# Queries and keys of a hybrid decoder layer written straight to both heads' operands, and the first attention weights issued among the first pair's projections

## The chip, the cores and the metric

One NeuronCore of a Trainium2 chip runs the kernel. The metric is the device time of one execution in microseconds (us), shown as the median of three runs; one further execution was profiled.

## The reference, cut to what matters

One decoder layer on 1024 tokens with model width 1024, all in float32: a joint input projection whose columns feed a short gated convolution, stick-breaking attention (8 heads of 64) and a spatial gating unit; an output projection; a squared-ReLU MLP; a gated per-layer embedding. The change touches the attention alone:

```python
q = rms_norm(q.reshape(bsz, s_len, ATTN_HEADS, HEAD_DIM), q_norm_g[i])
k = rms_norm(k.reshape(bsz, s_len, ATTN_HEADS, HEAD_DIM), k_norm_g[i])
...
z = jnp.einsum('bqhd,bkhd->bhqk', qi, kj) * scale
log_beta = jax.nn.log_sigmoid(z)
log_rem = jnp.where(causal, jax.nn.log_sigmoid(-z), 0.0)
suffix = lax.cumsum(log_rem, axis=3, reverse=True) - log_rem
weights = jnp.where(causal, jnp.exp(log_beta + suffix), 0.0)
o = jnp.einsum('bhqk,bkhd->bqhd', weights, vj)
```

## The kernel before

**Precision.** Each float32 operand of a matmul is kept as a high part and a low part in the type float32r. A product of two such operands takes three matmuls (high by high, high by low, low by high; lines 161 to 163). Most work outside TensorE is the making of these parts: ScalarE casts the high part (line 134, or line 137 with a gain), VectorE subtracts it for the low part (line 135 or 138).

**Stages.** The kernel first brings the inputs and normalises them (the tiles xn), runs the gating unit's projection (`gating`, tiles vu_ps), then the attention's projections and the attention itself, mixed with one another and later with the convolution's projections (cv_ps); then the output projection (o_ps, from 410.7 us of the profile), the MLP (f_ps, d_ps) and the gate (g_ps). The heads go in four pairs. `project(pr)` makes q, k and v of one pair of heads: eight token tiles t of 128, each with 24 matmuls into the bank qkv_ps, then ScalarE and VectorE work (sum of squares ss, the root rs on GpSimd, the product qk, and V's two parts).

**Turning.** After each second tile `turn_qk` (lines 395 to 419) transposes q and k of two tiles and both heads into one PSUM bank qk_tr, head 0 on partitions 0 to 63 (lo_p), head 1 on 64 to 127 (hi_p). The operands that the attention wants, per head hh and half th of the tokens, are QS (q's high part on the head's own partitions, its low part on the other 64), KH (k's high part on both) and KL (k's low part on the head's own, zeros elsewhere), so that z = q k takes two matmuls with 128 rows each. Before the change the turn writes q's high part of both heads into QS[0], its low part into q_lo, k's high part into KH[0], and both KL. After the fourth tile of a half (t % 4 == 3) six joins move 64-partition pieces: three on ScalarE (lines 413 to 415), three on VectorE (lines 416 to 418). Until then neither head has its operands.

**Attention.** `attention()` yields 32 steps, for each pair head 0 with the token groups g = 0 to 3 and then head 1 with g = 3 to 0. A step has two parts. `stick` makes two tiles of weights: z by TensorE (lines 448, 450), a sigmoid by ScalarE into rem (line 452), a product scan along the keys by VectorE (line 457), and differences wt on VectorE or GpSimd (line 464); the lengths go from 128 to 1024 with the token tile, so the steps with g = 3 are the heavy ones, and they stand next to each other in the middle of a pair. `gather` transposes the weights (w_tr, line 486), splits them into wT_hi and wT_lo, and multiplies with V into the bank av (line 504). qk_tr, w_tr and a few others share a pool of three PSUM banks (ps_tr).

**Order.** The order of issue is written with generators: `weave` takes from the attention and from the next projections (`fill`) by their units of work, `later` delays a turn by 72 units. A scheduler of the Tile framework then moves instructions within an engine's queue; each engine runs its queue in order. Before the change the attention starts when `alone`, the gating unit and the first pair's projections, has been written out whole (lines 697 to 706).

Of the kernel before, what the change touches and what calls it, by code (L numbers as in the profile page):

```python
# [17 lines left out]
KT = D // P  # L18
# [15 lines left out]
def hybrid_block(ctx: ExitStack, tc: tile.TileContext, a: dict):  # L34
# [310 lines left out]
    def project(pr):  # L345
# [9 lines left out]
        low_q = [None, None]  # L355
        heads[pr] = QS, KH, KL, V, low_q
        for t in range(KT):
            th, ts = block(t)
            if t % 4 == 0:
                for hh, other in enumerate((hi_p, lo_p)):  # L360
                    KL[hh][th] = slot("KL", F32R)
                    nc.gpsimd.memset(KL[hh][th][other].bitcast(F32), 0.0)
                KH[0][th] = slot("KH", F32R)
                QS[0][th] = slot("QS", F32R)
                low_q[th] = slot("q_lo", F32R)
                QS[1][th] = slot("QS", F32R)
                KH[1][th] = slot("KH", F32R)
# [27 lines left out]
    def turn_qk(head, t, qk):  # L395

        QS, KH, KL, _, low_q = head
# [7 lines left out]

        split(tr[:, :256], QS[0][th][:, ws], low_q[th][:, ws], scale=gq)
        nc.scalar.activation(KH[0][th][:, ws], tr[:, 256:], AF.Copy, scale=gk)
        for hh, own in enumerate((lo_p, hi_p)):
            nc.vector.scalar_tensor_tensor(out=KL[hh][th][own, ws], in0=tr[own, 256:],
                                           scalar=gk[own], in1=KH[0][th][own, ws],  # L410
                                           op0=ALU.mult, op1=ALU.subtract)
        if t % 4 == 3:
            nc.scalar.copy(KH[1][th][hi_p], KH[0][th][hi_p])
            nc.scalar.copy(KH[1][th][lo_p], KH[0][th][hi_p])
            nc.scalar.copy(KH[0][th][hi_p], KH[0][th][lo_p])
            nc.vector.tensor_copy(QS[1][th][hi_p], QS[0][th][hi_p])
            nc.vector.tensor_copy(QS[1][th][lo_p], low_q[th][hi_p])
            nc.vector.tensor_copy(QS[0][th][hi_p], low_q[th][lo_p])
# [4 lines left out]
    def attend(pr):  # L423

        QS, KH, KL, V, _ = heads[pr]
# [203 lines left out]


# [67 lines left out]
    fill = stream(project(1), project(2), project(3), convolve())  # L698
    for _ in alone:
        pass  # L700
    attending = attention()
    for pr in range(4):
        while waiting:
            emitted[0] += waiting.pop(0)[1]()
        weave(attending, ATTEND + {0: AHEAD, 3: -AHEAD}.get(pr, 0), fill,
              PROJECT if pr < 3 else CONVOLVE * 0.72)
# [638 lines left out]
```

## Time and profile before

| | |
|---|---|
| median of three runs | 1207.83 us (1206.86 to 1211.2) |
| the profiled execution's own time | 1206.75 us |
| its span | 1205.0 us |
| TensorE's granted clock | at its full level in all 40 slices |
| TensorE busy | 1181.0 us, 98% |
| VectorE, ScalarE, GpSimd busy | 885.7, 595.5, 400.5 us |
| projections and attention, mixed | about 75 to 410 us |

The span is what the profiler saw from the first to the last instruction; the execution's own time is 1.75 us longer. A busy TensorE counts overlapping matmuls, so that its idle time is a lower bound of what it lost. Each view names, for an engine's idle time, the instruction that ended it ("releaser").

### The profile page before, as it was taken

The numbers are of one execution on the slowest core, as the hardware profiler recorded it, in microseconds if no ns is written. First come the engines' busy times: TensorE is split into PE (matmuls) and PEld (weight loads), VectorE is DVE, ScalarE is ACT, GpSimd is POOL, SyncE is SP. The second block draws the span as 40 slices with busy tenths as digits, with TensorE's granted clock in tenths as the row PEclk, the third lists the DMA queues.
The fourth block names the chain that finished last, engine by engine and source line by source line (L and its number), as shares of the span: only waits on it lengthen the run. The fifth ranks groups of instructions, "written<-read, shape, count | busy, mean of one in ns | idle before, by whom it ended". The sixth has DMA issues, their size and how long they took to land.

```text
span 1205.0 us, 17538 instructions
## 1 busy us (share of the span) xinstructions
PE 1181.0 (98%) x5788; PEld 1007.1 (84%) x5788; DVE 885.7 (73%) x1310; ACT 595.5 (49%) x1148; POOL 400.5 (33%) x472
## 2 busy tenths in 40 slices
PE   9999899998999999999999999999999999999997
PEld 7899899898888888888888888888888888888886
DVE  7846898989896667868877777787664657753697
ACT  7735565565643466733334333356543444456642
POOL 3324355464352222045354453421023301013412
PEclk9999999999999999999999999999999999999999
DMA  9602359999673776679998989777889975644857
GB/s 311 233 18 90 130 172 262 253 194 167 140 146 95 196 263 204 204 207 261 265 240 249 264 238 260 221 257 277 300 267 295 290 249 175 231 146 119 181 155 209
DMA packets 127963, 254.03 MB, mean 211 GB/s; under 512 B 14496, under 2 KB 22432, under 8 KB 127168
## 3 DMA queue, kind: packets, MB, share of 16 engines
q1 hardware_dynamic: 94992, 168.08, 41.4%
q0 software_dynamic: 27664, 57.05, 25.2%
q10 hardware_dynamic: 5216, 27.79, 6.4%
q8 instruction: 45, 0.74, 0.3%
q14 instruction: 46, 0.38, 0.1%
HBM read 192.30 MB, written 92.80 MB: 237 GB/s over the span
## 4 chain that ended last, share of the span: by engine, by line
PE 88%; DVE 8%; ACT 1%; issue 1%; DMA 1%; POOL 1%; SPq 0%; DVEq 0%; ACTq 0%; POOLq 0%
PE f_ps L814 25%; PE d_ps L814 25%; PE g_ps L814 6%; DVE rem L457 3%; PE qkv_ps L161 3%; PE qkv_ps L162 2%; PE qkv_ps L163 2%; PE o_ps L161 2%; PE o_ps L163 2%; PE o_ps L162 2%; PE av L504 2%; PE cv_ps L163 2%; PE cv_ps L161 2%; PE cv_ps L162 2%; PE w_tr L486 1%; PE vu_ps L162 1%
## 5 line engine op out<-in xcount | busy, mean ns | idle before, releaser
L135 DVE TENSOR_TENSOR w_lo<-raw,w_hi 128x512 fp32r<-128x512 f32 x280 | 243.1, 872 | 85.0 <-ACT w_hi L134 83.1
L134 ACT CAST w_hi<-raw 128x512 fp32r<-128x512 f32 x280 | 172.5, 620 | 240.5 <-PE d_ps L814 115.4
L814 PE MATMUL f_ps<-hn_hi,w_hi 128*128 128x512 f32 x448 | 175.2, 392 | 0.0
L814 PE MATMUL f_ps<-hn_lo,w_hi 128*128 128x512 f32 x448 | 174.9, 390 | 0.0
L814 PE MATMUL d_ps<-f_hi,w_hi 128*128 128x512 f32 x448 | 174.8, 390 | 0.0
L814 PE MATMUL f_ps<-hn_hi,w_lo 128*128 128x512 f32 x448 | 174.6, 391 | 0.0
L814 PE MATMUL d_ps<-f_hi,w_lo 128*128 128x512 f32 x448 | 174.3, 389 | 0.0
L814 PE MATMUL d_ps<-f_lo,w_hi 128*128 128x512 f32 x448 | 174.3, 389 | 0.0
L457 DVE TENSOR_TENSOR_SCAN rem<-rem,after 128x128 f32<-128x128 f32 (+3 forms) x64 | 90.9, 1431 | 13.3 <-ACT rem L452 13.3
L814 PEld LDWEIGHTS f_ps<-hn_lo,w_hi 128*128 128x128 f32 x448 | 84.5, 189 | 17.9 <-issue 0.2
L814 PEld LDWEIGHTS f_ps<-hn_hi,w_hi 128*128 128x128 f32 x448 | 84.5, 189 | 17.8 <-issue 0.2
L814 PEld LDWEIGHTS f_ps<-hn_hi,w_lo 128*128 128x128 f32 x448 | 84.5, 189 | 17.6
L814 PEld LDWEIGHTS d_ps<-f_hi,w_hi 128*128 128x128 f32 x448 | 84.1, 188 | 17.7 <-issue 0.2
L814 PEld LDWEIGHTS d_ps<-f_hi,w_lo 128*128 128x128 f32 x448 | 84.1, 188 | 17.6
L814 PEld LDWEIGHTS d_ps<-f_lo,w_hi 128*128 128x128 f32 x448 | 84.1, 188 | 17.5 <-issue 0.2
L161 PE MATMUL qkv_ps<-whi,xn_hi 128*128 128x384 f32 x256 | 88.8, 347 | 0.9 <-DVE V L138 0.8
L162 PE MATMUL qkv_ps<-wlo,xn_hi 128*128 128x384 f32 x256 | 86.6, 338 | 0.0
L163 PE MATMUL qkv_ps<-whi,xn_lo 128*128 128x384 f32 x256 | 86.3, 337 | 0.0
L135 DVE TENSOR_TENSOR f_lo<-raw,f_hi 128x512 fp32r<-128x512 f32 x112 | 78.2, 728 | 8.5 <-ACT f_hi L134 8.2
L134 ACT CAST f_hi<-raw 128x512 fp32r<-128x512 f32 x112 | 67.1, 620 | 25.6 <-DMA raw<-f_dram 21.6
L800 POOL TENSOR_TENSOR S<-S,sq 128x512 f32<-128x512 f32 x19 | 25.6, 1347 | 160.1 <-ACT sq L876 160.1
L452 ACT ACTIVATE rem<-z 128x128 f32<-128x128 f32 (+3 forms) x96 | 46.7, 500 | 24.3 <-PE z L450 21.6
(250 smaller groups left out, 2618.9 us busy)
## 6 DMA issues: line engine op xcount, KB each, us to landing
raw<-in_w_ff SPq DMA_DIRECT2D x148, 256.0 KB, 4.2
raw<-f_dram SPq DMA_DIRECT2D x112, 256.0 KB, 5.1
raw<-w_sums SPq DMA_DIRECT2D x64, 256.0 KB, 4.1
f_dram<-f SPq DMA_DIRECT2D x48, 256.0 KB, 3.9
f_dram<-t SPq DMA_DIRECT2D x48, 256.0 KB, 4.0
w_sums<-in_w_ff POOLq DMA_DIRECT2D x8, 1024.0 KB, 12.1
w_sums<-w_sums POOLq DMA_DIRECT2D x8, 1024.0 KB, 15.3
raw<-in_w_out SPq DMA_DIRECT2D x28, 256.0 KB, 3.5
```

Source lines behind the costliest of these rows:

```text
L134: last_hi[0] = nc.scalar.copy(hi, src)
L135: low.tensor_tensor(out=lo, in0=src, in1=hi, op=ALU.subtract)
L161: nc.tensor.matmul(ps, lh, rh, start=first and i == 0, stop=False)
L162: nc.tensor.matmul(ps, lh, rl, start=False, stop=False)
L163: done = nc.tensor.matmul(ps, ll, rh, start=False, stop=last and i == len(terms) - 1)
L452: last_act[0] = nc.scalar.activation(rem[:, ks], z, AF.Sigmoid, scale=-HD ** -0.5)
L457: nc.vector.tensor_tensor_scan(out=back, data0=back, data1=after[:, T - W:][:, ::-1], initial=1.0, op0=ALU.mult, op1=ALU.max)
L486: nc.tensor.transpose(tr[:, n:n + P], wts[i][:, kb * P:(kb + 1) * P], ident)
L504: nc.tensor.matmul(av[:, first * P:], lhs, part[:, o:o + m], start=kb == 0 and part is hi, stop=kb == 2 * g + 1 and part is lo)
L800: return eng.tensor_tensor(out=out, in0=x, in1=y, op=ALU.add)
L814: done = nc.tensor.matmul(bank, l, r, start=first and k == 0 and i == 0, stop=k == len(b) - 1 and i == 2, skip_group_check=True)
```

## The change

The q and k parts are written by six ScalarE and four VectorE instructions per turn, each on the 64 partitions of one head, straight to the places where the attention reads them: for each head q's high part to QS's own half, k's high part to KH's own half, q's low part to QS's other half, k's low part to KL, and k's high part once more to KH's other half. The tile q_lo and the six joins are gone. The first step's `stick` (26 units) is taken when 100 units of the first pair's projections are left, instead of behind them, and `weave`'s totals follow.

```diff
--- before.py
+++ after.py
@@ -352,19 +352,16 @@
         KH = [[None, None], [None, None]]
         KL = [[None, None], [None, None]]
         V = [None] * 4
-        low_q = [None, None]
-        heads[pr] = QS, KH, KL, V, low_q
+        heads[pr] = QS, KH, KL, V
         for t in range(KT):
             th, ts = block(t)
             if t % 4 == 0:
                 for hh, other in enumerate((hi_p, lo_p)):
                     KL[hh][th] = slot("KL", F32R)
                     nc.gpsimd.memset(KL[hh][th][other].bitcast(F32), 0.0)
-                KH[0][th] = slot("KH", F32R)
-                QS[0][th] = slot("QS", F32R)
-                low_q[th] = slot("q_lo", F32R)
-                QS[1][th] = slot("QS", F32R)
-                KH[1][th] = slot("KH", F32R)
+                for hh in range(2):
+                    QS[hh][th] = slot("QS", F32R)
+                    KH[hh][th] = slot("KH", F32R)
             ps = bank(ps_mm, "qkv_ps")[:, :384]
             for k0 in range(0, KT, 2):
                 product(ps, [(cols(xn[k][th], ts), wk[k]) for k in (k0, k0 + 1)],
@@ -394,7 +391,7 @@
 
     def turn_qk(head, t, qk):
 
-        QS, KH, KL, _, low_q = head
+        QS, KH, KL, _ = head
         th = t // 4
         tr = bank(ps_tr, "qk_tr")
         for i in range(2):
@@ -402,27 +399,22 @@
                 o = j * 256 + i * P
                 nc.tensor.transpose(tr[:, o:o + P], qk[:, i, j * P:(j + 1) * P], ident)
         ws = slice((t % 4 - 1) * P, (t % 4 + 1) * P)
-
-        split(tr[:, :256], QS[0][th][:, ws], low_q[th][:, ws], scale=gq)
-        nc.scalar.activation(KH[0][th][:, ws], tr[:, 256:], AF.Copy, scale=gk)
-        for hh, own in enumerate((lo_p, hi_p)):
-            nc.vector.scalar_tensor_tensor(out=KL[hh][th][own, ws], in0=tr[own, 256:],
-                                           scalar=gk[own], in1=KH[0][th][own, ws],
-                                           op0=ALU.mult, op1=ALU.subtract)
-        if t % 4 == 3:
-            nc.scalar.copy(KH[1][th][hi_p], KH[0][th][hi_p])
-            nc.scalar.copy(KH[1][th][lo_p], KH[0][th][hi_p])
-            nc.scalar.copy(KH[0][th][hi_p], KH[0][th][lo_p])
-            nc.vector.tensor_copy(QS[1][th][hi_p], QS[0][th][hi_p])
-            nc.vector.tensor_copy(QS[1][th][lo_p], low_q[th][hi_p])
-            nc.vector.tensor_copy(QS[0][th][hi_p], low_q[th][lo_p])
+        for hh, (own, other) in enumerate(((lo_p, hi_p), (hi_p, lo_p))):
+            q, k = tr[own, :256], tr[own, 256:]
+            nc.scalar.activation(QS[hh][th][own, ws], q, AF.Copy, scale=gq[own])
+            nc.scalar.activation(KH[hh][th][own, ws], k, AF.Copy, scale=gk[own])
+            nc.vector.scalar_tensor_tensor(out=QS[hh][th][other, ws], in0=q, scalar=gq[own],
+                                           in1=QS[hh][th][own, ws], op0=ALU.mult, op1=ALU.subtract)
+            nc.vector.scalar_tensor_tensor(out=KL[hh][th][own, ws], in0=k, scalar=gk[own],
+                                           in1=KH[hh][th][own, ws], op0=ALU.mult, op1=ALU.subtract)
+            nc.scalar.activation(KH[hh][th][other, ws], k, AF.Copy, scale=gk[own])
         return 8
 
     PROJECT = KT * 72 + 32
 
     def attend(pr):
 
-        QS, KH, KL, V, _ = heads[pr]
+        QS, KH, KL, V = heads[pr]
         yb = y_kept if pr == 3 else None
         if pr == 3:
             y_kept.extend(halves("y_b"))
@@ -627,6 +619,8 @@
             if t % 4 == 3:
                 later(250, lambda th=th, vp=vp, vu=vus: mix(th, vp, vu))
 
+    GATING = 2 * (4 * KT * 12 + 1 + 24 + 16)
+
 
     y_a = []
 
@@ -696,13 +690,18 @@
         pass
     alone = stream(gating(), project(0))
     fill = stream(project(1), project(2), project(3), convolve())
+
+    for _ in take(alone, GATING + PROJECT - 100):
+        pass
+    attending = attention()
+    for _ in take(attending, AHEAD):
+        pass
     for _ in alone:
         pass
-    attending = attention()
     for pr in range(4):
         while waiting:
             emitted[0] += waiting.pop(0)[1]()
-        weave(attending, ATTEND + {0: AHEAD, 3: -AHEAD}.get(pr, 0), fill,
+        weave(attending, ATTEND - (AHEAD if pr == 3 else 0), fill,
               PROJECT if pr < 3 else CONVOLVE * 0.72)
     y = [[], []]
 
```

The scheduler makes more of this than the diff tells. Three places show it. In all rows the number behind a tile's name tells tiles of one name apart.

On TensorE, in the first pair's projections (qkv_ps, 24 matmuls a tile), behind the fifth of their eight tiles: before, the transposes of the third and fourth tile (qk_tr) are followed by the sixth tile's projections, and the first z stand behind the seventh tile.

```order
L163 MATMUL qkv_ps_1161<-whi_945,xn_lo_524 128x384
L403 MATMUL qk_tr_1186<-ident,qk_1062 128x128 x4
L161 MATMUL qkv_ps_1214<-whi_903,xn_hi_462 128x384
L162 MATMUL qkv_ps_1214<-wlo_904,xn_hi_462 128x384
L163 MATMUL qkv_ps_1214<-whi_903,xn_lo_463 128x384
```
```order
L163 MATMUL qkv_ps_1249<-whi_945,xn_lo_524 128x384
L448 MATMUL z_1349<-KH_953,QS_954 128x128
L450 MATMUL z_1349<-KL_949,QS_954 128x128
L448 MATMUL z_1422<-KH_953,QS_954 128x256
L450 MATMUL z_1422<-KL_949,QS_954 128x256
L403 MATMUL qk_tr_1274<-ident,qk_1209 128x128 x2
```

Now:

```order
L163 MATMUL qkv_ps_1164<-whi_945,xn_lo_524 128x384
L440 MATMUL z_1278<-KH_954,QS_953 128x128
L442 MATMUL z_1278<-KL_949,QS_953 128x128
L400 MATMUL qk_tr_1189<-ident,qk_1061 128x128 x2
L440 MATMUL z_1287<-KH_954,QS_953 128x256
L442 MATMUL z_1287<-KL_949,QS_953 128x256
L400 MATMUL qk_tr_1189<-ident,qk_1061 128x128 x2
L161 MATMUL qkv_ps_1216<-whi_903,xn_hi_462 128x384
```

The first z of head 0 moved from behind the seventh tile to behind the fifth, in among the transposes of the third and fourth tile, whose joins they no longer need.

On TensorE, in the first pair's heavy steps, around the transposes of head 0's longest weights (w_tr of wt_1587 before, wt_1586 now): before, no projection stands in the 24 rows between their own z and them; the last two z in that piece, shown here, are head 1's.

```order
L448 MATMUL z_1722<-KH_957,QS_1159 128x512
L450 MATMUL z_1722<-KL_951,QS_1159 128x512
L486 MATMUL w_tr_1735<-ident,wt_1587 128x128
L486 MATMUL w_tr_1735<-ident,wt_1568 128x128
L486 MATMUL w_tr_1735<-ident,wt_1587 128x128
L486 MATMUL w_tr_1750<-ident,wt_1587 128x128
L486 MATMUL w_tr_1750<-ident,wt_1568 128x128
L486 MATMUL w_tr_1750<-ident,wt_1587 128x128
L448 MATMUL z_1835<-KH_1160,QS_1159 128x128
L450 MATMUL z_1835<-KL_1154,QS_1159 128x128
L448 MATMUL z_1839<-KH_957,QS_1159 128x512
L450 MATMUL z_1839<-KL_951,QS_1159 128x512
```

Now 20 projections of one tile, 12 matmuls of av, four z of head 1 and four more projections stand between head 0's z and these transposes; the end of that piece:

```order
L442 MATMUL z_1675<-KL_1158,QS_1162 128x384
L440 MATMUL z_1679<-KH_956,QS_1162 128x512
L442 MATMUL z_1679<-KL_951,QS_1162 128x512
L163 MATMUL qkv_ps_1623<-whi_1427,xn_lo_397 128x384
L161 MATMUL qkv_ps_1623<-whi_1433,xn_hi_429 128x384
L162 MATMUL qkv_ps_1623<-wlo_1434,xn_hi_429 128x384
L163 MATMUL qkv_ps_1623<-whi_1433,xn_lo_430 128x384
L400 MATMUL qk_tr_1705<-ident,qk_1530 128x128 x2
L478 MATMUL w_tr_1739<-ident,wt_1567 128x128
L478 MATMUL w_tr_1754<-ident,wt_1567 128x128
L478 MATMUL w_tr_1739<-ident,wt_1586 128x128
L478 MATMUL w_tr_1739<-ident,wt_1567 128x128
```

Projections (qkv_ps) moved in between the heavy steps; head 1's longest z moved behind the transposes.

On VectorE, at the same place, the turn of the second pair's first two tiles, with the instruction ahead of it:

```order
L457 SCALAR_TENSOR_TENSOR rem_1586<-rem_1586,after 128x1024
L138 SCALAR_TENSOR_TENSOR q_lo_1410<-qk_tr_1672,c_gq,QS_1409 128x256
L384 TENSOR_TENSOR qk_1704<-qkv_ps_1709,rs_1783 128x256
L464 TENSOR_TENSOR wt_1587<-rem_1586 128x1023
L457 SCALAR_TENSOR_TENSOR rem_1684<-rem_1684,after 128x896
L409 SCALAR_TENSOR_TENSOR KL_1404<-qk_tr_1672,c_gk,KH_1408 64x256
L409 SCALAR_TENSOR_TENSOR KL_1406<-qk_tr_1672,c_gk,KH_1408 64x256
```

Now:

```order
L135 TENSOR_TENSOR wT_lo_1745<-w_tr_1739,wT_hi_1744 128x512
L406 SCALAR_TENSOR_TENSOR QS_1441<-qk_tr_1705,c_gq,QS_1441 64x256
L408 SCALAR_TENSOR_TENSOR KL_1437<-qk_tr_1705,c_gk,KH_1442 64x256
L135 TENSOR_TENSOR wT_lo_1760<-w_tr_1754,wT_hi_1759 128x512
L381 TENSOR_TENSOR qk_1727<-qkv_ps_1623,rs_1725 128x256
L449 SCALAR_TENSOR_TENSOR rem_1692<-rem_1692,after 128x1024
L406 SCALAR_TENSOR_TENSOR QS_1443<-qk_tr_1705,c_gq,QS_1443 64x256
L408 SCALAR_TENSOR_TENSOR KL_1439<-qk_tr_1705,c_gk,KH_1444 64x256
```

The turn has two halves, one per head, with other work between them; a scan of 1024 moved between the halves, and the difference wt of 1023 out of them.

## Rows read from the trace of the kernel before

**Rows 1.** The page, part 1: busy time and instructions of each engine.
```profile
PE 1181.0 (98%) x5788; PEld 1007.1 (84%) x5788; DVE 885.7 (73%) x1310; ACT 595.5 (49%) x1148; POOL 400.5 (33%) x472
```

**Rows 2.** What TensorE waited for, 85 to 400 us: total us, times, longest.
```profile
PE w_tr L486 <- DVE KL L409: 3.6, 4, 1.5
PE w_tr L486 <- DVE wt L464: 3.2, 3, 1.6
PE av L504 <- DVE wT_lo L135: 2.9, 4, 1.8
PE qk_tr L403 <- DVE qk L384: 1.5, 1, 1.5
```

**Rows 3.** Busy time by stretch of 20 to 25 us: first stretch, sum of all fifteen.
```profile
85.00:110.00 25.00, 25.00 (x157) 24.87 (x156) 12.44 (x33) 10.05 (x26) 6.17 (x9) 1.00 0.06 22
...
sum 305.00, PE 291.68 PEld 268.61 DVE 258.22 ACT 165.83 POOL 145.30; mean PE 19.45 PEld 17.91 DVE 17.21 ACT 11.06 POOL 9.69
```

**Rows 4.** Busy time in three stretches with the longest scans, and in a calm one.
```profile
129.60:166.00 36.40, 32.98 (x206) 30.21 (x205) 32.02 (x41) 18.35 (x44) 12.51 (x15) 1.00 0.36 123
196.00:232.40 36.40, 33.86 (x215) 31.26 (x213) 32.45 (x42) 18.78 (x45) 17.52 (x18) 1.00 0.95 244
261.00:298.00 37.00, 33.72 (x211) 31.10 (x212) 33.07 (x42) 19.38 (x47) 16.93 (x20) 1.00 1.03 190
...
232.40:261.00 28.60, 28.56 (x193) 27.74 (x193) 25.72 (x47) 19.31 (x51) 20.48 (x33) 1.00 0.85 207
```

**Rows 5.** Timeline of TensorE, 140 to 152 us: start, length, what ended idle time.
```profile
141.96 0.60 PE L403 MATMUL qk_tr<-ident,qk 128*128 128x128 f32 x4
...
147.02 0.88 PE L486 MATMUL w_tr<-ident,wt 128*128 128x128 f32 x6 [1.64 <-DVE wt L464]
...
149.93 0.63 PE L486 MATMUL w_tr<-ident,wt 128*128 128x128 f32 x4 [0.94 <-DVE KL L409]
```

**Rows 6.** VectorE's groups by form, 85 to 400 us: busy us, mean ns, idle before.
```profile
L135 DVE TENSOR_TENSOR wT_lo<-w_tr,wT_hi 128x512 fp32r<-128x512 f32 x48 | 32.1, 680 | 3.4 <-ACT wT_hi L134 2.7
...
L457 DVE TENSOR_TENSOR_SCAN rem<-rem,after 128x1024 f32<-128x1024 f32 x8 | 19.2, 2403 | 1.7 <-ACT rem L452 1.7
...
L409 DVE SCALAR_TENSOR_TENSOR KL<-qk_tr,c_gk,KH 64x256 fp32r<-64x256 f32 x32 | 15.3, 479 | 1.5 <-ACT KH L407 1.1
L384 DVE TENSOR_TENSOR qk<-qkv_ps,rs 128x256 f32<-128x256 f32 x31 | 12.9, 415 | 8.9 <-POOL rs L170 8.7
...
L464 DVE TENSOR_TENSOR wt<-rem 128x1023 f32<-128x1023 f32 x8 | 10.5, 1312 | 0.0
...
L138 DVE SCALAR_TENSOR_TENSOR q_lo<-qk_tr,c_gq,QS 128x256 fp32r<-128x256 f32 x16 | 7.5, 471 | 0.6 <-ACT QS L137 0.5
...
L416 DVE CAST QS<-QS 64x512 fp32r<-64x512 f32 x8 | 3.4, 421 | 0.0
```

**Rows 7.** Timeline of VectorE, 80 to 150 us: the first scans, and one KL pair.
```profile
111.21 1.01 DVE L457 TENSOR_TENSOR_SCAN rem<-rem,after 128x128 f32<-128x128 f32 x2 [1.16 <-ACT rem L452]
...
117.19 2.54 DVE L457 TENSOR_TENSOR_SCAN rem<-rem,after 128x384 f32<-128x384 f32 x2
119.77 1.13 DVE L464 TENSOR_TENSOR wt<-rem 128x511 f32<-128x511 f32 x1
...
148.82 0.97 DVE L409 SCALAR_TENSOR_TENSOR KL<-qk_tr,c_gk,KH 64x256 fp32r<-64x256 f32 x2
```

**Rows 8.** What VectorE waited for, 85 to 400 us: total us, times, longest.
```profile
DVE rem L457 <- ACT rem L452: 13.3, 11, 2.5
...
DVE wT_lo L135 <- ACT wT_hi L134: 7.8, 14, 2.6
```

**Rows 9.** ScalarE's groups by form, 85 to 400 us: busy us, mean ns, idle before.
```profile
L137 ACT ACTIVATE QS<-qk_tr,c_gq 128x256 fp32r<-128x256 f32 x16 | 7.7, 483 | 0.5 <-PE qk_tr L403 0.3
...
L413 ACT CAST KH<-KH 64x512 fp32r<-64x512 f32 x8 | 4.9, 617 | 0.2
...
L521 ACT COPY av_lo<-av 64x256 f32<-64x256 f32 x7 | 2.6, 370 | 7.7 <-PE av L504 7.6
```

## Prediction

> **What bounds the kernel now.** The page comes first. TensorE is busy for 98% of the span [rows 1], so the time can only change where TensorE waits, or where its work changes. Its work doesn't change: the same matmuls stand in another order. The waits of TensorE come next, taken for the stretch in which the diff acts, 85 to 400 us [rows 2]. All four large ones name VectorE: the weights' transposes w_tr wait 3.6 us for KL, which holds a PSUM bank until k's low part is out, and 3.2 us for the differences wt; av waits 2.9 us for wT_lo, and qk_tr 1.5 us for qk. The table by stretches bounds the whole: from 85 to 390 us TensorE is busy for 291.68 of 305.00 us, so 13.3 us of idle time is there [rows 3]. Three stretches, one in the middle of each of the first three pairs of heads, hold 3.4, 2.5 and 3.3 of them, 9.2 together: there the longest scans stand next to each other, and VectorE is busy for 88 to 89% [rows 4]. The calm stretch beside them lost 0.04 us. The timeline shows how one such stretch stops: TensorE transposes q and k at 141.96, waits 1.64 us for wt, then 0.94 us for KL, which ends at 149.79 [rows 5, 7]. That is 7.2 us behind the end of the transposes at 142.56, because VectorE runs a scan and a difference in between. So the reader should see a TensorE that is full except where VectorE comes too late, in three places of some 37 us.
>
> **The change part by part.**
>
> *VectorE's instructions.* Away go 16 q_lo of 0.471 us, 32 KL of 0.479 and 24 joins; the three kinds of join move the same 64x512 and one stands for all, 0.421 [rows 6]. That is 7.5 + 15.3 + 10.1 = 32.9 us. Instead come 64 instructions of 64x256. KL has this form already, 0.479, and its 128x256 sister q_lo is no slower for twice the partitions; writing to the other 64 partitions is what two of the three joins did. So 64 x 0.479 = 30.7, and VectorE saves **2.2 us**. If the price were off by 5% either way, it would be 0.7 to 3.7.
>
> *ScalarE's instructions.* Away go 32 of 128x256 with a gain, 0.483 each, and 24 casts of 0.617 [rows 9], 15.5 + 14.8 = 30.3 us. Instead come 96 of 64x256 with a gain. No row shows that form: a plain copy of 64x256 takes 0.370, and the 128x256 form with a gain 0.48. I take 0.48, as the nearer operation, hence 46.1 us; from below it is 35.5. ScalarE gets 5 to 16 us more. It is busy for 165.8 of 305 us [rows 3], so this alone binds nothing. Its cover is its own idle time; where that isn't to be had, VectorE waits longer for rem and wT_hi, for which it waits 13.3 and 7.8 us now [rows 8].
>
> *The earlier start.* Without joins, the weights of the first two tiles need only the first turn, and the order puts their z behind the fifth tile of projections instead of the seventh. In 85 to 110 us VectorE is busy for 12.44 of 25 us [rows 3]: the scans of the first two groups and their one difference on VectorE, 1.01 + 2.54 + 1.13 = 4.7 us [rows 7], which now run at 111 to 121 us, find room there. VectorE has **4.7 us** less to do afterwards. The bounds are 0, if TensorE stops for other things at the same places, and 4.7. I take the whole, since every large wait of TensorE behind 110 us names VectorE. The z cost nothing there: TensorE computes them anyway.
>
> *The turn in two halves.* Within a turn ScalarE must now make k's second copy of the first head, then q and k of the second, 3 x 0.48 = 1.44 us, before VectorE can go on with the second head. The scheduler filled that gap in eleven of the sixteen turns with scans, differences or parts of weights of about that length or more (the most frequent of them, a wT_lo, takes 0.680 [rows 6]). In five it left one qk of 0.415 or nothing. Two of these lie before 110 us, where VectorE has time; in the other three VectorE stands for about 1.0 us, **3.0 us** in all. Bounds: 0, if ScalarE's other work had VectorE waiting there already, and 16 x 1.44 = 23 if it is late in every turn; ScalarE is 54% busy, so the low end is nearer.
>
> *The bank of qk_tr.* It is free when ScalarE and VectorE have read it. In the heavy stretch of the second pair's first turn the chain now is two ScalarE instructions (0.96), two on VectorE (0.96), wT_lo, qk and a scan of 1024 (0.680 + 0.415 + 2.403), two more on VectorE (0.96): 6.4 us at least, and a last copy on ScalarE behind. The old chain, which took the measured 7.2 us, comes by the same kind of sum to 6.0 at most: 0.48 and 0.47, qk, a wt of 1.312, a scan of 896 that is no longer than the one of 1024, and 0.96. So the bank is held at least 0.35 us longer. Taking three such places I set **1.0 us**. The bounds are minus 3.6, the whole of today's wait for KL, and plus 15, the rival below. The turn also adds a wait: ScalarE's last copy of k for each head now stands behind VectorE's KL. Queued behind it stand sigmoids of z and casts of w_tr, for which VectorE's scans and wT_lo wait; I price that with the halves above. The transfers are the same; in SP's queue a few stores of the attention's output and loads of the next weights change places, and POOL's first differences come earlier, into its idle time: nothing for either.
>
> *Sum:* -2.2 - 4.7 + 3.0 + 1.0 = -2.9 us. The profiled execution took 1206.75 us, which gives 1203.85; the median of the runs is 1.08 us above it, which gives **1204.9 us**.
>
> **A rule weighed.** By TensorE's own rows the three heavy stretches can give back 9.2 us. The Trainium skill (Perfetto Trace Analysis, section Identifying the Most-Contended Engine) holds that the share of busy matmuls is no good measure for TensorE, since matmuls overlap, and asks for the busy share of the weight loads. The trace bears that out in part: loads are busy for 27.74 of 28.60 us in the calm stretch, 97%, and for 30.21, 31.26 and 31.10 of 36.4, 36.4 and 37.0 us in the heavy ones [rows 4]. By that rule these could shrink to 31.1, 32.2 and 32.1 us, an estimate of 14.4 us to be had in place of 9.2; the faster rival would then end at 1193.4.
>
> **The rivals.**
>
> *The waits vanish.* The order puts projections between the heavy steps where none stood: 20 projections, 12 av and more between head 0's longest z and its transposes. If TensorE thus never waits for wt or KL in the three stretches, all 9.2 us go: 1207.83 - 9.2 = **1198.6 us**. For it: the waits come from missing cover, and the cover is now in the queue. Against it: VectorE's work in these stretches hardly falls, and it was busy for 88%; a projection issued there is missing later.
>
> *The bank is held too long.* A turn now goes from ScalarE to VectorE and back five times instead of four, with the last reader on ScalarE: 0.48 for the second head's start, 0.96 for the second half, 0.48 for the last copy, some 1.9 us longer wherever neither engine is free. In four of today's turns TensorE already waits for KL [rows 2]; there nothing covers the addition, 4 x 1.9 = 7.6 us. If half of it is uncovered in the eight others behind the first pair, that is another 7.6. Less the 6.9 us that VectorE is spared, the kernel is 8.3 us slower: **1216.1 us**. It decides from the point where TensorE's work between the transposes and the next tile in the same bank is shorter than the hold. For it: the hold is 7.2 us in the heavy place. Against it: the scheduler moved other work into the gaps, and half of the turns stand where TensorE has long runs of projections.
>
> *The change does little.* TensorE waits for the same late scans, and the early start only moves VectorE's idle time from 100 to 130 us. Then 4.7 falls away and the sum is +1.8: 1209.6 us. This lies within what can't be told from no change.
>
> **How the numbers follow.** A measurement of this kernel tells a change from none at about 0.5%, 6 us. I give the forecast with its small companion, within 6 us either way, 0.52; the vanishing waits 0.29; the held bank 0.19. The likeliest is 1204.9 us, with 1201.9 to 1209.6 as its own range. The range for 8 in 10 reaches down nearly to the full 9.2 us, with a little for the rule's larger estimate, to 1197.0, and up to three quarters of the slower rival, 1213.5.
>
> **What would show it.** Right: the first scan starts some two tiles of projections earlier than 111.2 us; VectorE busy for 2 us less, ScalarE for about 16 more; TensorE's idle time from 85 to 390 us at 9 to 11 us instead of 13.3, with the wait for wt smaller and a wait for KL or KH still there. The stages behind 411 us should keep their lengths and start about 3 us earlier. Wrong: w_tr waiting 8 us or more for KL or KH (the slower rival), or TensorE's three stretches with less than 1 us of idle time each (the faster one); or a change behind 411 us, which no step here gives.

## The result and the profile after

Over 20 runs of each kernel the change takes 1210.8 us (median; 1208.4 to 1213.3) and the kernel before 1208.2 us (1206.0 to 1211.2). The ratio is 1.0021, with a 95% interval of 1.0013 to 1.0029: slower by 0.2%, some 2.6 us. The forecast was 1204.9 us, 2.9 us faster than before. The profiled execution of the change took 1210.48 us, of before 1206.75 us.

The page, part 1, of the change, to be held against [rows 1]:

```profile
PE 1182.5 (98%) x5788; PEld 1008.2 (83%) x5788; DVE 884.6 (73%) x1302; ACT 602.6 (50%) x1188; POOL 403.4 (33%) x472
```

VectorE is spared 1.1 us, ScalarE has 7.1 us more, TensorE's work is the same. The timelines of TensorE say where the time went. First of before, then of the change, the first matmul of the output projection:

```profile
410.71 0.39 PE L161 MATMUL o_ps<-y_hi,wo_hi 128*128 128x512 f32 x1
```
```profile
414.54 0.47 PE L161 MATMUL o_ps<-y_hi,wo_hi 128*128 128x512 f32 x1 [0.87 <-DVE cv_acc L657]
```

It starts 3.8 us later, and the span is 3.8 us longer (1208.8 against 1205.0): all of the loss lies in the stretch in which the change acts, and what follows takes 794.3 us in both. The whole of that stretch, 85 to 400 us, by busy time (columns as in [rows 3]), first before, then the change:

```profile
85.00:400.00 315.00, 301.68 (x1848) 277.02 (x1847) 261.45 (x398) 169.00 (x406) 148.74 (x201) 1.00 0.67 163
```
```profile
85.00:400.00 315.00, 300.52 (x1840) 276.07 (x1839) 256.72 (x389) 176.12 (x443) 147.47 (x200) 1.00 0.66 163
```

TensorE's idle time here grew from 13.3 to 14.5 us, at full clock in both. From 400 us to the output projection it has none in before and 1.0 us in the change. So 2.1 of the 3.8 us are idle time of TensorE; the other 1.7 us lie in rows that count as busy, and were not traced. What it waited for in the change, 85 to 415 us (total us, times, longest), beside [rows 2]:

```profile
PE qkv_ps L161 <- DVE V L138: 5.8, 9, 1.1
PE w_tr L478 <- DVE wT_lo L135: 2.7, 3, 1.6
PE qk_tr L400 <- DVE qk L381: 1.8, 2, 1.5
PE z L440 <- ACT rem L444: 1.3, 1, 1.3
PE av L496 <- ACT wT_hi L134: 1.1, 2, 0.7
PE w_tr L478 <- DVE wt L456: 0.9, 1, 0.9
PE o_ps L161 <- DVE cv_acc L657: 0.9, 1, 0.9
...
PE w_tr L478 <- ACT KH L410: 0.2, 1, 0.2
```

The two waits that the prediction set out from are nearly gone: w_tr for KL, 3.6 us before, and w_tr for wt, 3.2 before, 0.9 now; the late reader of that bank is KH, with 0.2. In their place stands a wait that before had only twice, for 0.8 us: a projection waits for its own bank, qkv_ps, of which there are two. V's low part on VectorE is the bank's last reader, and it follows V's high part on ScalarE. One such place, in timelines of VectorE, ScalarE and TensorE of the change, 142 to 150 us:

```profile
145.43 2.29 DVE L449 TENSOR_TENSOR_SCAN rem<-rem,after 128x1024 f32<-128x1024 f32 x1 [0.37 <-ACT rem L444]
147.75 0.49 DVE L406 SCALAR_TENSOR_TENSOR QS<-qk_tr,c_gq,QS 64x256 fp32r<-64x256 f32 x1
148.25 0.49 DVE L408 SCALAR_TENSOR_TENSOR KL<-qk_tr,c_gk,KH 64x256 fp32r<-64x256 f32 x1
148.78 0.35 DVE L138 SCALAR_TENSOR_TENSOR V<-qkv_ps,r,V 128x128 fp32r<-128x128 f32 x1
```
```profile
145.42 0.47 ACT L405 ACTIVATE KH<-qk_tr,c_gk 64x256 fp32r<-64x256 f32 x1
145.92 0.37 ACT L137 ACTIVATE V<-qkv_ps,r 128x128 fp32r<-128x128 f32 x1
146.18 0.58 ACT L134 CAST wT_hi<-w_tr 128x512 fp32r<-128x512 f32 x1
148.78 0.47 ACT L410 ACTIVATE KH<-qk_tr,c_gk 64x256 fp32r<-64x256 f32 x1 [2.02 <-DVE KL L408]
```
```profile
149.18 0.45 PE L161 MATMUL qkv_ps<-whi,xn_hi 128*128 128x384 f32 x1 [1.10 <-DVE V L138]
```

The head's KH is ready at 145.89, but VectorE has begun a scan of 2.29 us at 145.43. Behind it stand the turn's two subtractions, and only then V's low part, whose input, the high part, is ready since 146.29; TensorE stops 1.10 us, and ScalarE's second copy of k stops for 2.02. So it goes in most of the nine places. In eight of them V's high part was out 0.66 us or more before VectorE began the low part; directly ahead of it on VectorE stood a turn's QS and KL (five places) or a scan (three). One of the latter, ScalarE's V and then VectorE:

```profile
214.83 0.37 ACT L137 ACTIVATE V<-qkv_ps,r 128x128 fp32r<-128x128 f32 x1
```
```profile
215.24 2.29 DVE L449 TENSOR_TENSOR_SCAN rem<-rem,after 128x1024 f32<-128x1024 f32 x1
217.56 0.35 DVE L138 SCALAR_TENSOR_TENSOR V<-qkv_ps,r,V 128x128 fp32r<-128x128 f32 x1
```

So V is late mostly by VectorE's own queue. In only three of the nine had VectorE, in the half of a turn just before, stood for ScalarE's KH (1.06, 0.50 and 0.18 us). What the two engines waited for in all, 85 to 411 us; VectorE of the change, then ScalarE of before and of the change:

```profile
DVE QS L406 <- ACT KH L405: 9.9, 11, 1.8
...
DVE rem L449 <- ACT rem L444: 6.9, 8, 2.1
```
```profile
ACT V L137 <- DVE qk L384: 20.6, 15, 3.8
...
ACT KH L407 <- DVE q_lo L138: 9.0, 10, 3.7
```
```profile
ACT V L137 <- DVE qk L381: 40.4, 17, 5.3
ACT KH L410 <- DVE KL L408: 18.0, 21, 2.0
```

VectorE now stands 9.9 us, eleven times, for ScalarE (its wait for rem fell from the 13.3 of [rows 8] to 6.9), and ScalarE stands longer for VectorE. Four of the eleven, 4.5 us, stand ahead of a turn's first half, and seven, 5.4 us, between its halves. Behind 110 us the longest between halves are these three; the other two are 0.16 and 0.18 us:

```profile
161.56 0.49 DVE L406 SCALAR_TENSOR_TENSOR QS<-qk_tr,c_gq,QS 64x256 fp32r<-64x256 f32 x1 [1.05 <-ACT KH L405]
...
193.77 0.49 DVE L406 SCALAR_TENSOR_TENSOR QS<-qk_tr,c_gq,QS 64x256 fp32r<-64x256 f32 x1 [0.50 <-ACT KH L405]
...
229.73 0.49 DVE L406 SCALAR_TENSOR_TENSOR QS<-qk_tr,c_gq,QS 64x256 fp32r<-64x256 f32 x1 [1.05 <-ACT KH L405]
```

### The profile page after: what moved, and what is told of

It reads as the page before. It is cut to its first block, busy times and chain, and to the rows that moved or that the text cites. A ratio compares the mean times of both kernels' runs of the same rounds, so it can differ in the third digit from the quotient of the medians.

```text
span 1208.8 us, 17563 instructions
## 1 busy us (share of the span) xinstructions
PE 1182.5 (98%) x5788; PEld 1008.2 (83%) x5788; DVE 884.6 (73%) x1302; ACT 602.6 (50%) x1188; POOL 403.4 (33%) x472
## 4 chain that ended last, share of the span: by engine, by line
PE 83%; DVE 8%; issue 3%; ACT 3%; DMA 1%; POOL 1%; SPq 0%; ACTq 0%; DVEq 0%; POOLq 0%
PE f_ps L813 25%; PE d_ps L813 25%; PE g_ps L813 6%; DVE rem L449 3%; PE o_ps L161 2%; PE o_ps L163 2%; PE o_ps L162 2%; PE qkv_ps L161 2%; PE qkv_ps L162 2%; PE qkv_ps L163 2%; PE av L496 2%; PE w_tr L478 1%; PE vu_ps L161 1%; PE vu_ps L162 1%; PE vu_ps L163 1%
## 5 line engine op out<-in xcount | busy, mean ns | idle before, releaser
L135 DVE TENSOR_TENSOR w_lo<-raw,w_hi 128x512 fp32r<-128x512 f32 x280 | 252.8, 906 | 90.8 <-ACT w_hi L134 88.2
L170 POOL TENSOR_TENSOR rs<-ss,mhalf 128x4 f32<-128x4 f32 x32 | 44.0, 1376 | 71.2 <-DVE ss L376 71.2
```

What stands on the lines that cost most here:

```text
L135: low.tensor_tensor(out=lo, in0=src, in1=hi, op=ALU.subtract)
L170: last_power[0] = nc.gpsimd.tensor_tensor(out=out, in0=in_, in1=mhalf[:, :n], op=ALU.pow)
```

## The experiments

Theory A: the direct writes make the two engines wait for each other within the turns, V comes late, and projections wait for its bank. Theory B: the earlier start and its order cost. Theory C: the 64-partition instructions cost by themselves, whatever bank is waited for. Theory D came from the first eight runs: the scheduler draws a new order after any edit, and the draw alone is worth this much. Ratios are to runs of before taken alongside (their medians lie from 1208.3 to 1209.4 us), with 95% intervals, so that they differ a little from quotients of the times given.

### One part of the change, one bank more, V first

**The writes alone.** The diff against the change:
```diff
-    for _ in take(alone, GATING + PROJECT - 100):
-        pass
-    attending = attention()
-    for _ in take(attending, AHEAD):
-        pass
     for _ in alone:
         pass
+    attending = attention()
```
(and the weave's totals as before.)

> Before is 1208.2 us, the change 1210.8. This kernel has the direct writes, but the attention starts where it started before. Theory A (a new wait: a projection's bank of qkv_ps comes free late, because V's high part stands on ScalarE behind the turns, which the writes in two halves made longer): the loss belongs to the writes, so 1211 to 1213, later than the change by what the earlier start gave, and the waits of TensorE for V's low part are there, some 8 of them and 4 to 6 us. Theory B (the loss belongs to the earlier start and the order that it brings): 1206 to 1208.5, as before or faster, and those waits are at most 3.

Measured: 1211.6 us, ratio 1.0018 (1.0006 to 1.0030), about the change's own time. And the first scan on VectorE starts at 102.11, as in the change (102.39), not at the 111.21 of [rows 7]:

```profile
102.11 1.01 DVE L449 TENSOR_TENSOR_SCAN rem<-rem,after 128x128 f32<-128x128 f32 x2 [1.17 <-ACT rem L444]
```

So the writes alone let the scheduler bring the first weights forward, since no join holds them; where the program writes them isn't needed for that. Theory B's forecast missed, but the early start stands in this kernel too, so that it is not told apart from the writes. Theory A's waits aren't here either: z for rem 3.7 us, av for wT_hi 4.7, and V only 1.5. And the like time has another source. The whole stretch, and a part of it behind a stop of 2.98 us:

```profile
85.00:400.00 315.00, 302.77 (x1829) 280.14 (x1829) 255.22 (x387) 176.62 (x441) 151.13 (x199) 0.98 0.66 161
```
```profile
214.00:220.00 6.00, 5.83 (x20) 5.13 (x20) 5.69 (x9) 2.73 (x7) 1.03 (x1) 0.50 1.13 206
```

TensorE is idle for 12.2 us, less than the 13.3 of before; what it loses against before shows in the granted clock, 0.98 over the stretch and 0.50 in places, where before and the change have 1.00.

**The start alone** (before's joins, the change's main part):

> Before with its joins, and only the attention's start moved forward. Theory A: the start gives what was forecast, 1203.5 to 1206, and TensorE's waits for V's low part stay near 1 us. Theory B: 1210 to 1213, with those waits as in the change (5.8 us, 9 times), although no turn is longer.

Measured: 1222.6 us, 1.0112 (1.0090 to 1.0133). This kernel doesn't compute what the reference asks for (where it departs was not traced), though it has as many instructions on each engine as before. The first scan starts at 112.0 us, no earlier than in before, so it didn't bring the early start that it was to test, and its time decides nothing. What the early start is worth by itself stays untested.

**A third bank for projections:**
```diff
-    ps_mm = front.enter_context(tc.tile_pool(name="ps_mm", bufs=2, space=PSUM))
+    ps_mm = front.enter_context(tc.tile_pool(name="ps_mm", bufs=3, space=PSUM))
-    ps_tr = front.enter_context(tc.tile_pool(name="ps_tr", bufs=3, space=PSUM))
+    ps_tr = front.enter_context(tc.tile_pool(name="ps_tr", bufs=2, space=PSUM))
```


> The change with a third bank for the projections, taken from the transposes' pool (qk_tr and w_tr keep two). Theory A: the wait for V's low part goes (under 1 us), 1205 to 1208 if the transposes do with two banks; waits of w_tr and qk_tr for their bank can eat 1 to 3 us of it. Theory B and theory C (the turns' 64-partition instructions cost by their own length and waits, whatever bank is waited for): 1210 to 1212, the waits only change names.

Measured: 1233.3 us, 1.0202 (1.0181 to 1.0223), a miss for every theory. The wait for V's low part, which theory A had gone, is 5.8 us as in the change (3 times, the longest 3.4). With two banks the transposes come late; VectorE, 85 to 411 us, now waits for them before it may write the next differences, a wait that is in none of the lists above:

```profile
DVE wt L456 <- PE w_tr L478: 16.9, 8, 5.3
```

Taking the third bank from the transposes costs far more than it gives the projections.

**V first** (in `project`, the same lines moved):
```diff
+            if t % 2 == 0:
+                V[t // 2] = slot("V", F32R, (P, 2, 2, 2, HD))
+            v = V[t // 2][:, t % 2]
+            split(ps[:, 256:].rearrange("p (h d) -> p h d", d=HD), v[:, :, 0], v[:, :, 1], scale=r1[t])
             sq = half_tmp("qk_sq", (P, 4, HD + 1))
```


> The change with V's two instructions written ahead of the sums of squares and of qk, so that a projection's bank is given back by qk and not by V. Theory A: TensorE's waits for the projection's bank fall from 5.8 us to 2 or less and the time is 1206 to 1208.5. Theory C: the waits for V go, but qk comes later by V's 0.4 us on ScalarE and on VectorE, and qk_tr waits instead: 1210 to 1212.

Measured: 1208.5 us, 0.9996 (0.9983 to 1.0008): the loss is gone. The waits for the bank fell from 5.8 to 1.6 us, now for qk:

```profile
PE w_tr L478 <- DVE wT_lo L135: 5.3, 3, 2.9
...
PE qkv_ps L161 <- DVE qk L385: 1.6, 2, 1.1
```

This is what theory A said, though w_tr's wait for wT_lo doubled (2.7 to 5.3).

### The turns, V first elsewhere, and more work for ScalarE

**Copies ahead of subtractions** (in the change; the six ScalarE copies of a turn are written before its four VectorE instructions):
```diff
-        for hh, (own, other) in enumerate(((lo_p, hi_p), (hi_p, lo_p))):
+        sides = list(enumerate(((lo_p, hi_p), (hi_p, lo_p))))
+        for hh, (own, other) in sides:
...
+            nc.scalar.activation(KH[hh][th][other, ws], k, AF.Copy, scale=gk[own])
+        for hh, (own, other) in sides:
```


> The change, with a turn's six ScalarE copies ahead of its four VectorE instructions, so that the two engines no longer take turns (VectorE's wait for KH, 9.9 us in 11 times, and ScalarE's wait for KL, 18.0 us in 21, should both fall). Theory A (V's high part is late because ScalarE is held up in the turns): ScalarE gets to V sooner, TensorE's waits for the projection's bank fall to 3 us or less, 1206.5 to 1209. Theory C (what costs is VectorE's waiting within the turns): also faster, 1206 to 1208, but with TensorE's waits for V still there. If neither holds: 1210 to 1212.

Measured: 1224.6 us, 1.0123 (1.0107 to 1.0139), a miss. VectorE waits longer for KH than in the change, not less, and one wait of TensorE for the output's copy y_both took 7.0 us:

```profile
DVE QS L410 <- ACT KH L407: 18.3, 13, 2.6
```
```profile
PE av L499 <- ACT y_both L508: 7.4, 2, 7.0
```

**Before, V first:**

> Before, with joins, but V's two instructions ahead of the sums of squares and of qk. Theory A: before waits for this bank only twice (0.8 us), so there is nothing to win: 1207.5 to 1210. If V first wins 2 us or more here as well (under 1206.5), then it is worth something of its own, and that it wins 2.3 us in the change says nothing of why the change lost.

Measured: 1212.0 us, 1.0027 (1.0015 to 1.0040): with joins V first loses 3.2 us, where in the change it won 2.3.

**Both edits in the change:**

> The change with both: copies ahead of subtractions, and V first. Theory A: both act on the same wait, so little beyond V first alone (1208.5): 1206.5 to 1209. If they act on different waits, the gains add: 1204 to 1207.

Measured: 1214.2 us, 1.0045 (1.0032 to 1.0059). Slower than expected, but V first won 10.4 us over the regrouped kernel.

**Before, with two more copies per turn:**
```diff
+        for own in (lo_p, hi_p):
+            nc.scalar.activation(KH[0][th][own, ws], tr[own, 256:], AF.Copy, scale=gk[own])
         if t % 4 == 3:
```


> Before with its joins, and in each turn two more ScalarE copies of 64 partitions, behind VectorE's two instructions and waiting for them, which write again what stands in KH already (nothing else changes). It gives ScalarE of the turns the change's hold-up without the change. Theory A: V's high part gets late as in the change, TensorE waits for the projection's bank 4 us or more, 1210 to 1213. If 14 us more of ScalarE and the wait cost nothing, as the prediction had it: 1207.5 to 1209.

Measured: 1230.3 us, 1.0177 (1.0162 to 1.0192). The 32 copies take 32 x 0.470 = 15 us of an engine that is idle nearly half the time, and the kernel is 21.5 us slower. The copies' group on ScalarE, and TensorE's largest waits:

```profile
L413 ACT ACTIVATE KH<-qk_tr,c_gk x32: 460/470/475, 96.5 to 349.2; 64x256 fp32r<-64x256 f32 x32
```
```profile
PE qkv_ps L161 <- DVE V L138: 8.5, 6, 1.7
PE av L506 <- DVE wT_lo L135: 8.2, 8, 2.1
```

So in this kernel the added copies were not free, and the wait of theory A came with them. The copies do more than take time, though: they wait for VectorE, they hold the bank qk_tr until they are done (w_tr waits 1.0 us for them), and they bring another order; how much each is worth was not told apart. The size is beyond theory A, and so is that of the copies ahead of subtractions. Each of these edits had moved some hundreds of TensorE's instructions by the scheduler, which led to theory D.

### The draw of the order

**A neutral swap, in before and in the change.** In the projection, on ScalarE:
```diff
-            nc.scalar.copy(sq[:, :, HD], ms1e[t].broadcast_to([P, 4]))
             nc.scalar.activation(sq[:, :, :HD], ps[:, :256].rearrange("p (h d) -> p h d", d=HD),
                                  AF.Square, scale=HD ** -0.5)
+            nc.scalar.copy(sq[:, :, HD], ms1e[t].broadcast_to([P, 4]))
```


> Before, with one pair of ScalarE instructions swapped per projection (the 128x4 copy of the constant column behind the squares instead of ahead of them). Work, data and waits are the same; the scheduler draws another order from it (257 of TensorE's 5637 rows move). Theory A (the change lost by V's bank): the order of rows as such is worth nothing much, 1207.5 to 1210. Theory D (any edit in this stretch makes the scheduler draw a new order, and a draw is worth 2 to 4 us either way, so the change's 2.6 us need no part of it that costs): off from before by 2 us or more, either way.

> The same swap in the change (819 of TensorE's 5639 rows move). Theory A: 1209.5 to 1212, as the change, with V's low part still waited for 4 us or more. Theory D: off from the change's 1210.8 by 2 us or more, either way, or the waits stand elsewhere at the same sum.

Measured: 1213.8 us, 1.0050 (1.0033 to 1.0067), and 1217.0 us, 1.0070 (1.0052 to 1.0088): +5.4 on before, +6.2 on the change, for a swap that leaves out and adds nothing. Theory D holds: a new order by itself can be worth more than the whole result. Much of it is the clock. The runs of the swap in before have a mean granted clock of 0.992, those of before alongside 0.995; at the rate found in the last section (5.6 us for 0.004) this is about 5 us, an estimate, nearly all of the 5.4. What one bad place of it costs is seen there.

**Another rule of the scheduler** (`schedule_with_timeline_sim=False` in both):

> Before, ordered by the framework's scheduler without its modelled timeline: other rules, and another order in all engines (987 TensorE rows move). No forecast of its own time; it is the partner of the next.

> The change, ordered in the same way as the run before this one. Theory A: the direct writes lengthen ScalarE's turns in any order, so slower than its partner, by 1 to 4 us, with more waits for V's low part. Theory D: the difference can have either sign and need not be near 2.6 us.

Measured: 1288.95 us, 1.0668 (1.0647 to 1.0690), and 1301.8 us, 1.0777 (1.0752 to 1.0802). The change is 12.8 us slower here, and waits for V rise from 5.3 to 11.9 us.

**Turns 54 and 90 units behind the projection** (one number, `later(72, ...)`, in both):

> Before, with the turns written out 54 units of work behind their projection instead of 72 (308 of TensorE's 5637 rows move). Theory D: before's order is a good draw among those that such edits give, so 2 us or more above it, 1210 to 1215, and not under 1206. If before is an ordinary draw: as likely faster as slower.

> The change, with turns 54 units behind. Theory D: against its partner (the run before this one) anywhere from 4 us faster to 6 us slower, no steady cost of the writes to be seen. Theory A, by the pairs so far (2.6, 3.2 and 12.8 us slower, 3.5 us faster with V first): slower than its partner, by 2 to 4 us.

> Before, with the turns 90 units behind their projection (570 TensorE rows move). Theory D: 1210 to 1215, not under 1206, as the run with 54.

> The change, with turns 90 units behind (926 TensorE rows move). Theory D: from 4 us faster than its partner to 6 us slower. Theory A: slower than its partner by 2 to 4 us.

Measured: 1208.8 us, 1.0004 (0.9990 to 1.0018); 1211.6 us, 1.0026 (1.0011 to 1.0041); 1206.4 us, 0.9990 (0.9976 to 1.0003); 1214.4 us, 1.0044 (1.0029 to 1.0058). Before is thus no rare draw among such orders. The change is behind its partner both times, by 2.7 and 7.9 us. But the last run shows that theory A's wait isn't the only way the loss shows. TensorE's largest waits in the change with 90, where V's wait is small and the loss largest:

```profile
PE w_tr L478 <- DVE wt L456: 4.3, 3, 2.1
PE av L496 <- DVE wT_lo L135: 3.7, 4, 1.6
PE av L496 <- ACT wT_hi L134: 2.5, 2, 2.0
...
PE qkv_ps L161 <- DVE V L138: 0.9, 1, 0.9
```

**V first and 90 units, in both:**

> Before, with V's two instructions first and the turns 90 units behind. The partner of the next run. Theory A: with joins nothing is won by V first, so 1206 to 1211, not under the 1206.4 of 90 units alone.

> The change, with V's two instructions first and the turns 90 units behind. Theory A: V first takes V out from behind ScalarE's longer turns, so faster than the 1214.4 of the change with 90 units by 2 us or more, and the pair changes sign as it did at 72 units: faster than its partner by 1 to 4 us, 1204 to 1209. If the pair at 72 units was a draw (theory D): as likely slower than its partner as faster, 1208 to 1216.

Measured: 1205.4 us, 0.9966 (0.9952 to 0.9979), and 1208.6 us, 0.9997 (0.9982 to 1.0012). V first wins 5.7 us in the change, as theory A expected, but also 1.0 in before (2.9 by the ratios), where theory A had nothing to win; and the pair keeps its sign, +3.2 us, which theory A had the other way. The kernel before with these two edits is faster than both kernels, by 0.34% and 0.55%. TensorE, VectorE and ScalarE in it, 85 to 400 us:

```profile
85.00:400.00 315.00, 304.85 (x1871) 282.02 (x1870) 260.49 (x402) 167.28 (x407) 147.11 (x203) 1.00 0.67 164
```

TensorE is idle for 10.2 us, where before has 13.3.

### What the pairs say together

| edit in both | before, us | change, us | ratio of the ratios |
|---|---|---|---|
| none | 1208.2 | 1210.8 | 1.0021 |
| neutral swap | 1213.8 | 1217.0 | 1.0020 |
| turns at 54 | 1208.8 | 1211.6 | 1.0022 |
| turns at 90 | 1206.4 | 1214.4 | 1.0054 |
| V first | 1212.0 | 1208.5 | 0.9969 |
| V first, turns at 90 | 1205.4 | 1208.6 | 1.0031 |

The change is slower in five of six, by 0.2% in the mean (1.17% / 6), and slower under the other scheduler rule as well. Each ratio is uncertain by about 0.2%, so a steady cost alone would hardly run from -0.31 to +0.54%: each order adds its own amount, of the size of the result or more. A steady cost of about 0.2% would fit the sign, but the six scatter by 0.28%, which leaves their mean uncertain by 0.11% as a standard error (an estimate), and zero isn't excluded: it is not shown. The clock has its share here too. Of the twelve kernels, five have a granted clock of 1.00 from 85 to 400 us in their profiles: before, the change, and before with turns at 54, at 90, and at 90 with V first; the other seven, five of them with the change, have 0.98 or 0.99.

If there is a steady part, the turns in two halves are a candidate, by a difference that holds in all of the table's traces: VectorE waits 7.7 to 11.7 us for ScalarE within the turns of the change, and 1.6 to 5.3 us within those of before (for QS and KH together). It is not isolated: no kernel was found that takes away this wait and keeps the order. How much of the 2.6 us is the writes, how much the early start and how much the order stays open.

## Why the prediction was wrong

**Waits of w_tr for KL and wt would shrink:** right, from 6.8 us together to 0.9, with 0.2 for KH behind KL. The rival of the held bank did not come. Nor did that of the vanishing waits: they moved to other instructions.

**VectorE's instructions, -2.2 us:** right in size. KL and QS take 0.483 us each, 30.9 us for 64 against 32.9.

**The earlier start, -4.7 us:** the scan moved as said, from 111.21 to 102.39. TensorE's idle time from 110 to 150 us fell from 4.8 to 1.5 us, but from 150 to 400 us it rose from 8.5 to 12.2. The first transposes of weights came no earlier than before (116.2 against 114.9).

**The step that failed** is what these two terms were taken to be worth: the 6.9 us that VectorE is spared came off the time in full, for the start "since every large wait of TensorE behind 110 us names VectorE", and no term asked what TensorE would wait for next. From 85 to 400 us VectorE was in fact busy for 4.7 us less (256.7 against 261.5), and TensorE's waits for KL and wt fell by 5.9 us; but its idle time rose. The wait for the projections' own bank, for which the prediction had no term, went from 0.8 to 5.8 us, because V's low part stands behind the turns and scans in VectorE's queue; w_tr's wait for wT_lo went from 0.3 to 2.7. The prediction's own lower bound for the start, 0, "if TensorE stops for other things at the same places", is what the sum needs: without the 4.7 it gives 1209.6. That the start is worth nothing by itself was not isolated.

**ScalarE's instructions, 5 to 16 us more, priced at nothing.** The amount was right: 96 instructions at 0.461 to 0.470 make 44.8 us against 30.3, so 14.5 more; busy time rose by only 7.1 over the span, where consecutive instructions overlap (in the rows above, wT_hi starts at 146.18 while V ends at 146.29). The Trainium skill (ScalarE: Activation LUTs, section What ACT_TABLE_LOAD costs) gives about 93 ns of overlap between back-to-back instructions, and these two rows, with 110 ns, agree. "This alone binds nothing" was read from ScalarE's busy share of 54%, which is no ground for a price of nothing: fifteen us more of the same copies, in before, came with 21.5 us. What the 14.5 us cost in the change itself isn't shown, since V's high part was out in time at eight of the nine places.

**The turn in two halves, +3.0 us, three waits of 1.0.** Right: between the halves, behind 110 us, the three waits are 1.05, 0.50 and 1.05 us, 2.6 together. What the term left out are the 4.5 us that VectorE stands ahead of first halves, where the bank's first copies on ScalarE come late, and the reader that is late with VectorE: it named rem and wT_hi, but the one that TensorE waited for was V's low part.

**The bank of qk_tr, +1.0:** 0.2 for KH, so oversized.

The companion case, that the early start only moves idle time and the rest remains (1209.6), came closest to the measured 1210.8, but against a sum of waits that is made up otherwise: its nearness is in part luck. That the stages behind 411 us keep their lengths was right; they start 3.8 us later instead of 3 earlier. The wide range, 1197.0 to 1213.5, held the time; the forecast's own, 1201.9 to 1209.6, did not, and the sign was wrong. (Three quarters of the way to the slower rival would have been 1214.1, not 1213.5.)

## What to carry to other kernels

Work that one engine is spared doesn't come off the time in full because the other engine waits for it: ask which instruction it will wait for next, and what stands ahead of that one. Price work added to a half-idle engine by what stands behind it in its queue and whose buffer that frees, not by its busy share. When a scheduler orders the program, time the same edit in several orders before a result of some tenths of a per cent is put down to the edit: here one neutral swap moved the time by 5 us. Look at the granted clock of each order too: two kernels of the same time, here the change and the writes alone, can lose it in different ways. And where a bank has several readers, try the order of the readers: V first with the turns at 90 beat both kernels, though V first alone made before slower.

## What was not expected of the hardware

Stops of TensorE can be paid for twice. In the regrouped kernel it stops for 7.0 us at y_both. Its windows there (columns as in [rows 3]; the third figure from the end is the granted clock):

```profile
192.00:198.00 6.00, 6.00 (x38) 5.72 (x37) 5.52 (x11) 4.75 (x13) 4.49 (x9) 1.00 0.98 289
198.00:206.00 8.00, 1.00 (x6) 0.59 (x4) 2.27 (x3) 0.79 (x3) 0.00 (x0) 0.82 0.89 275
206.00:210.00 4.00, 3.99 (x16) 3.99 (x17) 3.74 (x5) 1.84 (x6) 2.11 (x1) 0.52 0.87 315
210.00:214.00 4.00, 4.00 (x27) 3.79 (x26) 1.75 (x3) 2.46 (x6) 4.00 (x5) 1.00 0.47 105
```

After the stop the clock is at its lower level, 1.2 GHz, almost all through the next 4 us: TensorE is busy, but gets through 16 instructions where the next window, at 2.4 GHz, has 27. The neutral swap in before shows the same behind a stop of 4.48 us for KL:

```profile
290.91 1.08 PE L486 MATMUL w_tr<-ident,wt 128*128 128x128 f32 x4 [4.48 <-DVE KL L409]
```
```profile
284.00:290.00 6.00, 1.66 (x11) 1.07 (x8) 6.00 (x4) 3.68 (x9) 4.02 (x4) 0.91 1.12 204
290.00:294.00 4.00, 3.09 (x11) 3.12 (x12) 3.95 (x7) 0.59 (x1) 0.00 (x0) 0.50 1.12 204
...
298.00:304.00 6.00, 6.00 (x47) 6.00 (x46) 4.80 (x8) 3.17 (x8) 3.02 (x4) 1.00 0.82 150
```

The Trainium skill (TensorE: Matmul & The Clock Gate, section HAM oscillation — how this bites in real kernels) tells of waits after which the next work starts at the lower clock; here the trace agrees, with waits for other engines in place of transfers. The stops needn't be as long as these two: in the writes alone a clock of 0.50 follows stops of 2.98 and 3.29 us, and one of 0.53 a stop of 1.68; yet a stop of 2.16 us, in before with turns at 54, was followed by the full clock. The loss of the change itself is not of this kind: its longest stop is 1.65 us, the clock is 1.00 from 85 to 400 us in both profiles, and its runs have the same mean clock as those of before, 0.996. But it widens what a draw of the order can cost, and it shows in repeated runs of before alone: those with a mean granted clock of 0.998 have a median of 1206.0 us, those with 0.994 one of 1211.6.
